# Inverting the 16x16 diagonal blocks of a chunked RWKV-7 recurrence: row by row over sixteen rows, or in two halves of eight

## The chip, the cores and the metric

The kernel runs on one core of one Trainium2 chip. The metric is the device time of one execution in microseconds (us), as the median of several runs. The engines are TensorE (PE; its weight loads are shown as PEld), VectorE (DVE), ScalarE (ACT), GpSimd (POOL) and SyncE (SP), which issues most of the DMAs.

## The reference

The model is a trunk of two layers over 1024 tokens of 1024 channels, all in float32. Layer 0 mixes tokens with a spatial-gating MLP, layer 1 with RWKV-7 time mixing; after each comes a squared-ReLU MLP of width 4096. Only the recurrence of layer 1 is touched here. For 16 heads of 64 channels it computes, token by token,

```
def step(S, inp):
    r_t, w_t, k_t, v_t, a_t, b_t = inp
    sa = einsum('bhij,bhj->bhi', S, a_t)
    S = S * w_t[..., None, :] + sa[..., None] * b_t[..., None, :] + v_t[..., None] * k_t[..., None, :]
    y = einsum('bhij,bhj->bhi', S, r_t)
    return S, y
```

The kernel does this in chunks of 64 tokens. Inside a chunk the tokens depend on each other through a strictly triangular 64x64 matrix L (for each head and chunk), and the chunk needs the inverse of I - L.

## The kernel before, in words

Channels lie on the 128 partitions, tokens along the free axis. The program runs the spatial-gating layer and its MLP, then the RWKV layer, then the last MLP. The products of the RWKV layer (projections to r, k, v, decay, gates, and the output projection) are taken a quarter of the tokens (256) at a time; weights come in pieces of 128x512 (SP queue, L260), are split into a high and a low part (wh: L285 on ACT and DVE; wl: L291 on DVE and POOL) and multiplied in `gemm_steps` (L803). Inputs of the products are mixes of neighbouring tokens (L787) that are split too (L321 on ACT, L324 on DVE).

Beside these products runs the recurrence (`wkv`). It has 16 units, one for each token quarter and pair of head pairs. A unit is made of stages, each a generator:

- A (`unit_a`) makes decay products, normalized keys (L1182, L1185), the operand `ar` (L1192) and, on PE, the grams (L1204); DVE masks them to `la` and `rr` (L1209). `la` holds L; it goes to a DRAM tile `ltd` (L1213).
- E (`unit_e`) transposes keys and values (L1228, L1238).
- S (`unit_s`, L1247 to L1276) inverts the 16x16 blocks on the diagonal of I - L. The 64 blocks of a unit (half of its 128) lie one to a partition, and in this layout S is work for DVE alone. It loads the blocks to `lb` (L1255) and then, for each row i from 2 to 15, multiplies column i of `lb` with the rows done so far into `pr` (L1263, i x i elements) and sums along the last axis into row i of `tb` (L1265). L1261 does row 1, L1267 makes the transposed copy. Two DMAs take `tb` to the DRAM tile `tpd` (L1271), and four bring it from there to the tiles `t` and `pf` (L1276).
- B (`unit_b`) goes from 16x16 to 32x32 and 64x64 blocks by small matmuls: L1300, a copy on ACT (L1306), L1312 and L1314, then L1319 on DVE and L1322 on ACT, L1329, copies L1334, L1340, copies L1344.
- C (`unit_c`) goes through the four chunks of the unit one after the other: L1366 and L1368, copy L1370, L1379, copies L1381, L1386, and L1394 on DVE, which makes the next state S. L1391 and L1392 make the output, D (`unit_d`) is the group norm (L1412 to L1427).

What stands in which order: each engine executes its instructions in program order and waits on semaphores. The steps of the generators are merged by due time (`interleave`): each yields a time in units, and the background products yield what they take; the table `RATES` says how much background goes beside a unit (20 to 20.6 for most, 8 for three of the last units). The framework then reorders what was emitted by its own estimate of when each instruction is ready. The yields of S run from 0.64 to 0.92, those of B start at 1.34 and those of C at 1.67.

Of the kernel before, what the change touches and what calls it, by code (L numbers as in the profile page):

```python
# [9 lines left out]
F32 = mybir.dt.float32  # L10
# [7 lines left out]
D = 1024  # L18
# [17 lines left out]
class Norm:  # L36
    """1 / rms of some tokens, the squares as the channels come, then what is made of it."""
# [36 lines left out]
    def ahead(self, n, e):  # L74
        """The normed values, to n."""
        self.n = n
        self.k.nc.vector.tensor_tensor(n[:, e], self.x[:, e], self.r, ALU.mult)


class Trunk:  # L80
# [16 lines left out]
    # ---------------------------------------------------------------- setup  # L97
# [18 lines left out]
    def mod(self, l, j):  # L116
        """Steps that make one adaLN vector of layer l, [128, 8], channel = chunk * 128 + partition."""
# [17 lines left out]
    def first_mods(self, l, js, hf):  # L135
        """The same for half of the vectors that all waits for, most of the sums on the tensor engine."""
# [23 lines left out]
    def ada_end(self, l, j, hf, ps):  # L160
        """Half a vector from sums along the free axis, the same on all partitions."""
# [11 lines left out]
    def ada_next(self, ahead=3):  # L173
        """The next block of ada_w; a later one is asked for ahead of its use."""
        while self.ada_todo and len(self.ada_got) < ahead:
            l, j, hf, k = self.ada_todo.pop(0)
            raw = self.aw.tile([P, 512], F32, name="araw", bufs=ahead + 1)
            self.last_ada = self.nc.sync.dma_start(raw, self.a["ada_w"][l, j, k, :, hf * 512:hf * 512 + 512])
            self.ada_got.append(raw)
        return self.ada_got.pop(0)  # L180
# [10 lines left out]
    def tick(self, n=1):  # L191
        """Emit n steps of the work that runs beside the products, norms first."""
# [8 lines left out]
    def flush(self):  # L201
        """Emit all steps of the norms."""
# [10 lines left out]
    # ---------------------------------------------------------------- pieces  # L213
    def acc(self):
        """A PSUM bank for a product."""
# [9 lines left out]
    def std(self, src):  # L225
        """A block of weights, half of the input channels at a time."""
        return [(src[:, h * 4:h * 4 + 4], 1, None) for h in range(2)]

    def stream(self, stop):
        """All weights in the order of use."""  # L230
# [40 lines left out]
    def split_piece(self):  # L271
        """Split weights: w = wh + wl exactly, each of 12 significant bits."""
# [23 lines left out]
    def prepare(self, n):  # L296
        """Have n split pieces ready."""
# [3 lines left out]
    def piece(self, ahead=None):  # L301
        """The next split piece; later ones are split, and others asked for, ahead of use."""
# [10 lines left out]
    def block(self):  # L313
        """The next two pieces, as high and low parts by input chunk."""
# [11 lines left out]
    def gemm(self, ps, w, x):  # L326
        """ps = w^T x, as wh xh + wh xl + wl xh."""
# [10 lines left out]
    # ---------------------------------------------------------------- SGU layer  # L338
# [35 lines left out]
    def v_weights(self, wx, ks):  # L374
        """The next split weights of v, for input chunks ks and half the channels."""
# [6 lines left out]
    def v_product(self, ps, h, tt, ks):  # L382
        """Half the channels of v for a token tile, from input chunks ks."""
# [5 lines left out]
    def sgu_begin(self, h, wx, mods, load):  # L389
        """The first products of v, of input chunks whose modulation is known, while mods makes the others'."""  # L390
# [14 lines left out]
    def sgu(self, h, sp, wx, ps0):  # L405
        """The gated product of both halves, split, in hp; h is let go."""
        nc = self.nc
        # v, tokens on partitions
# [5 lines left out]
        # half the channels at a time  # L414
# [26 lines left out]
        # u, channels on partitions; gating  # L441
# [26 lines left out]
    def sgu_out(self, x, ms, norms):  # L468
        """The output projection, one token half after the other."""
# [10 lines left out]
    # ---------------------------------------------------------------- MLP  # L480
    FB = FC // P

    # the hidden blocks that the first MLP takes last, the first token half before the second
# [8 lines left out]
    def mlp_pieces(self, l):  # L492
        """The weights of an MLP, but for the last of the first one."""
# [11 lines left out]
    def pairs(i):  # L505
        """How many pairs of output blocks the first MLP has left for before job i of the RWKV layer."""
# [30 lines left out]
    def mlp_block(self, l, x, h, fc, second=None):  # L537
        """One block of hidden channels. The first takes the first half of the tokens before the second, whose h
        is seen to by second(n), before step n."""
# [8 lines left out]
    def mlp_first(self, x, h, norms, second, last_up):  # L548
        """x += gate * MLP(h). norms is of what follows, by token half, and made along with the last of it;
        last_up comes when h is done with. Goes on as steps of two output blocks each."""  # L550
# [32 lines left out]
    def mlp_last(self, x, h, norms, second, last_up):  # L583
        """The same for the last layer, with norms by token range. last_up makes room for the weights of the last
        output blocks."""
# [18 lines left out]
    # ---------------------------------------------------------------- norms  # L604
    def modulated(self, l, j, hf, x, h):
        """Norm and modulation of a token half, split, to h[hf]."""
# [19 lines left out]
    def final(self, t0, x, last):  # L626
        """The output from token t0 on."""
# [17 lines left out]
    def prenorm(self, hf, x):  # L645
        """x and its norm for the RWKV layer, to DRAM; that of the first quarter also stays."""
# [15 lines left out]
    def rwkv_setup(self):  # L662
# [12 lines left out]
        # the norm of a key is taken of 2^-16 times its square  # L675
# [8 lines left out]
        # ones on the two diagonal 64-blocks, and what centres within a head  # L684
# [6 lines left out]
        # the same ones, rows scaled by r_k  # L691
# [3 lines left out]
        # gram masks [s, t]: s < t for the columns of alpha, s <= t for those of rho  # L695
        self.gmask = c.tile([P, 2, CS], F32, name="gmask")
        nc.gpsimd.memset(self.gmask, 1.0)
        # 0 for the rows of even 16-blocks, 1 for those of odd ones
# [12 lines left out]
        # 0 where a chunk starts  # L711
# [7 lines left out]
    # ---------------------------------------------------------------- RWKV: products of a token quarter  # L719
# [3 lines left out]
    def jobs(self):  # L723
        """The products in order: two blocks of 128 output channels, the hidden layer of a low-rank pair, or
        all of its outputs."""
# [10 lines left out]
    def parts(self):  # L736
        """The jobs before and beside the recurrence."""
# [5 lines left out]
    def pieces(self, jobs):  # L743
        """What the products take of the weights, in the order of use, half of the input channels at a time."""
# [30 lines left out]
    def mixes(self):  # L775
        """The token-shift mixes, split, one channel block at a time, in the order of use."""
# [17 lines left out]
    def gemm_steps(self, ps, x):  # L794
        """ps = w^T x in pieces, with the weights next in line."""
# [13 lines left out]
    def mix_set(self):  # L809
        """The next set of eight mixes; makes what is missing of it."""  # L810
# [5 lines left out]
    def ahead(self, n=1):  # L816
        """Make mixes of the next set."""
# [4 lines left out]
    def acc2(self):  # L822
        """A bank for two blocks."""
# [17 lines left out]
    def hidden(self, q, name, _):  # L841
# [15 lines left out]
        for m in (P, 96):  # L857
# [3 lines left out]
            # sigmoid(z) = 0.5 tanh(z / 2) + 0.5  # L861
# [38 lines left out]
    def gated(self, q, i):  # L900
        """What the output projection takes of a unit, split."""
# [8 lines left out]
    def outp(self, q, _, m):  # L910
        """Two blocks of the output projection of one token quarter, and the residual."""
# [27 lines left out]
    def last_outp(self, x, h, done=None):  # L939
        """Half of the output projection of the last token quarter, the first or the last four input chunks,  # L940
        added to x in place."""
# [16 lines left out]
    def rwkv_open(self):  # L958
        nc = self.nc
        N = self.N  # L960
        # first h of a token quarter, its step from token to token and small temporaries, then x of the first half
# [18 lines left out]
    def mt(self):  # L980
        """A small temporary."""
# [12 lines left out]
    def open_s(self):  # L994
        """For the hidden channels of an MLP, and h of the first quarter of the RWKV layer."""
# [4 lines left out]
    def rwkv(self, steps, before):  # L1000
        """The layer but for the output of the last quarter; the first steps of it beside those of steps."""
# [25 lines left out]
    # Chunk matrices in DRAM: rows of 64, a chunk every CB, so that 16-blocks on the diagonal follow at BB.  # L1027
# [599 lines left out]
```

## Time and profile before

| | |
|---|---|
| median of 3 runs | 2887.13 us (2882.05 to 2897.93) |
| the profiled execution, span from first to last instruction | 2884.1 us |
| PE busy in the span | 2724.9 us (94%) |
| DVE busy in the span | 1743.7 us (60%) |
| ACT busy, POOL busy | 1116.4 us (39%), 579.9 us (20%) |

The profile is of one execution, and for it the page shows no time but the span; the median of the runs is 3.0 us above that. "Busy" is the time in which an engine executes; a row of a view that ends in "<-" names what released the engine after it had been idle. The recurrence and its background products fill the stretch from about 1180 to 2110 us of the span. [...]

### The profile page before, as it was taken

The numbers are of one execution on the slowest core, as the hardware profiler recorded it, in microseconds if no ns is written. First come the engines' busy times: TensorE is split into PE (matmuls) and PEld (weight loads), VectorE is DVE, ScalarE is ACT, GpSimd is POOL, SyncE is SP. The second block draws the span as 40 slices with busy tenths as digits, with TensorE's granted clock in tenths as the row PEclk, the third lists the DMA queues.
The fourth block names the chain that finished last, engine by engine and source line by source line (L and its number), as shares of the span: only waits on it lengthen the run. The fifth ranks groups of instructions, "written<-read, shape, count | busy, mean of one in ns | idle before, by whom it ended". The sixth has DMA issues, their size and how long they took to land.

```text
span 2884.1 us, 48457 instructions
## 1 busy us (share of the span) xinstructions
PE 2724.9 (94%) x18858; PEld 2237.1 (78%) x18858; DVE 1743.7 (60%) x3315; ACT 1116.4 (39%) x2094; POOL 579.9 (20%) x568
## 2 busy tenths in 40 slices
PE   6999999999999998888899988998989999999998
PEld 4788888888888777777777777776778888888887
DVE  7856865433334577788888888677766333333335
ACT  4523432211222445445555555555454222122224
POOL 1000000000000033645544554554410000000002
PEclk9999999999999999888998989899999999999999
DMA  7644544111112446655555545545552111111112
GB/s 273 214 134 136 172 131 133 59 48 48 48 48 73 143 129 202 198 162 152 147 157 159 152 140 149 145 143 160 160 182 88 48 48 48 48 51 48 48 47 71
DMA packets 309414, 342.02 MB, mean 119 GB/s; under 512 B 150464, under 2 KB 165824, under 8 KB 308416
## 3 DMA queue, kind: packets, MB, share of 16 engines
q1 hardware_dynamic: 294208, 312.59, 36.0%
q10 hardware_dynamic: 14976, 26.34, 2.5%
q8 instruction: 148, 2.42, 0.3%
q14 instruction: 82, 0.67, 0.1%
HBM read 286.39 MB, written 52.45 MB: 117 GB/s over the span
## 4 chain that ended last, share of the span: by engine, by line
PE 73%; DVE 14%; DMA 4%; ACT 3%; issue 3%; POOL 1%; SPq 0%; DVEq 0%; ACTq 0%; POOLq 0%
PE acc L332 31%; PE acc L531 24%; PE acc L803 6%; PE acc L387 2%; DVE pr L1263 2%; DVE wl L291 2%; DVE xi L324 2%; DVE hm L787 2%; PE acc L888 1%; DVE ar L1192 1%; DMA araw<-in_ada_w 1%; PE g L1204 1%; PE m L1204 1%; DVE wh L285 1%; PE acc L952 1%
## 5 line engine op out<-in xcount | busy, mean ns | idle before, releaser
L332 PE MATMUL acc<-h,wh 128*128 128x512 f32 x2560 | 804.0, 395 | 0.6 <-ACT h L321 0.3
L285 ACT CAST wh<-raw 128x512 fp32r<-128x512 f32 (+1 forms) x589 | 362.5, 618 | 978.3 <-PE acc L531 533.2
L531 PE MATMUL acc<-s,wh 128*128 128x512 f32 (+1 forms) x2112 | 644.6, 387 | 0.6 <-DVE wh L285 0.6
L332 PEld LDWEIGHTS acc<-h,wh 128*128 128x128 f32 x2560 | 478.5, 188 | 114.4 <-DVE h L324 1.4
L291 DVE TENSOR_TENSOR wl<-raw,wh 128x512 fp32r<-128x512 f32 x524 | 379.1, 726 | 215.2 <-ACT wh L285 211.3
L332 PE MATMUL acc<-h,wl 128*128 128x512 f32 x1280 | 505.6, 395 | 0.0
L803 PE MATMUL acc<-xi,wh 128*128 128x256 f32 (+1 forms) x2176 | 469.9, 311 | 6.4 <-ACT xi L321 3.6
L531 PEld LDWEIGHTS acc<-s,wh 128*128 128x128 f32 x2112 | 393.2, 189 | 89.4 <-DVE s L323 0.9
L531 PE MATMUL acc<-s,wl 128*128 128x512 f32 (+1 forms) x1056 | 411.4, 390 | 0.5 <-DVE wl L291 0.5
L803 PEld LDWEIGHTS acc<-xi,wh 128*128 128x128 f32 (+1 forms) x2176 | 363.3, 202 | 32.9 <-issue 6.5
L336 DVE SCALAR_TENSOR_TENSOR x<-acc,mod,x 128x512 f32<-128x512 f32 (+1 forms) x232 | 165.1, 712 | 310.7 <-PE acc L531 294.5
L803 PE MATMUL acc<-xi,wl 128*128 128x256 f32 (+1 forms) x1088 | 325.0, 299 | 12.2 <-POOL wl L291 7.9
L291 POOL TENSOR_TENSOR wl<-raw,wh 128x512 fp32r<-128x512 f32 (+1 forms) x164 | 233.2, 1424 | 304.1 <-ACT wh L285 171.2
L332 PEld LDWEIGHTS acc<-h,wl 128*128 128x128 f32 x1280 | 240.6, 188 | 54.1 <-issue 0.5
L803 PEld LDWEIGHTS acc<-xi,wl 128*128 128x128 f32 (+1 forms) x1088 | 219.0, 201 | 17.4 <-POOL wl L291 8.9
L531 PEld LDWEIGHTS acc<-s,wl 128*128 128x128 f32 x1056 | 199.1, 189 | 42.9 <-DVE wl L291 1.2
L323 DVE CAST s<-relu 128x512 fp32r<-128x512 f32 x128 | 54.6, 426 | 224.1 <-ACT relu L519 224.1
L517 ACT ACTIVATE relu<-acc 128x512 f32<-128x512 f32 x128 | 76.0, 594 | 210.0 <-PE acc L332 210.0
L656 POOL TENSOR_SCALAR hq<-nt,mod,mod 128x256 f32<-128x256 f32 x8 | 5.9, 742 | 747.8 <-DVE nt L654 747.7
L640 POOL TENSOR_TENSOR hm<-hm,rstd 128x512 f32<-128x512 f32 x8 | 10.9, 1402 | 720.6 <-ACT rstd L638 720.6
L1263 DVE TENSOR_TENSOR pr<-lb,tb 64x4 f32<-64x4 f32 (+6 forms) x224 | 109.1, 487 | 3.1
L126 DVE SCALAR_TENSOR_TENSOR ada_acc<-araw,cond,ada_acc 128x512 f32<-128x512 f32 x140 | 104.3, 746 | 9.4 <-DMA araw<-in_ada_w 7.7
(233 smaller groups left out, 3570.1 us busy)
## 6 DMA issues: line engine op xcount, KB each, us to landing
raw<-in_mlp_w SPq DMA_DIRECT2D x304, 256.0 KB, 2.6
araw<-in_ada_w SPq DMA_DIRECT2D x192, 256.0 KB, 3.6
raw<-in_w_in SPq DMA_DIRECT2D x192, 256.0 KB, 3.1
raw<-in_b_w_out SPq DMA_DIRECT2D x64, 256.0 KB, 3.5
raw<-in_a_w_out SPq DMA_DIRECT2D x32, 256.0 KB, 2.8
raw<-in_w_v SPq DMA_DIRECT2D x24, 256.0 KB, 4.5
x<-in_x SPq DMA_DIRECT2D x4, 1024.0 KB, 6.9
raw<-in_w_u SPq DMA_DIRECT2D x16, 256.0 KB, 3.3
```

The source lines that it names most:

```text
L126: nc.vector.scalar_tensor_tensor(acc, raw, self.cond[:, k:k + 1], acc, ALU.mult, ALU.add)
L285: (nc.vector.tensor_copy if self.nhi % 3 == 0 and self.shared else nc.scalar.copy)(wh[:rows], raw[:rows])
L291: eng.tensor_tensor(wl[:rows], raw[:rows], rd(wh[:rows]), ALU.subtract)
L324: nc.vector.tensor_tensor(lo, src, rd(hi), ALU.subtract)
L332: nc.tensor.matmul(ps, w[s](k), x[m][:, k], start=n == 0, stop=n == 3 * KC - 1)
L336: self.nc.vector.scalar_tensor_tensor(x[:, e], ps, gate[:, e:e + 1], x[:, e], ALU.mult, ALU.add)
L387: self.nc.tensor.matmul(ps, h[s][:, k, ts], self.wv[k][m], start=k + i == 0, stop=k + i == KC + 1)
L517: nc.scalar.activation(r, ps, AF.Relu)
L531: nc.tensor.matmul(ps, w[:, k], s[hf, k][:, i, ts], start=n == 0, stop=n == 3 * FB - 1)
L787: nc.vector.scalar_tensor_tensor(t, self.hx[:, e], self.mu[:, i, e:e + 1], self.h[:, e, 1:], ALU.mult, ALU.add)
L803: nc.tensor.matmul(ps, s[:, k], xk[:, i], start=n == 0, stop=n == 23)
L1263: V.tensor_tensor(pr[:, :i, :i], lb[:, 0:i, i].unsqueeze(1).to_broadcast([64, i, i]), tb[:, 0, 0:i, 0:i].rearrange("p s k -> p k s"), ALU. ...
```

## The change

S is written in halves. The two 8x8 blocks on the diagonal of a 16x16 block are inverted together: for each row i from 2 to 7, one multiplication (L1275) of 2 x i x i elements and one sum (L1276). Then the 8x8 block below them is made as two products, each a multiplication of 8x8x8 = 512 elements (L1281, L1285) and a sum (L1283 into a new tile `wd`, L1287 into `tb`). Each unit so has 16 multiplications and sums where it had 28. The first copy (now L1272) and the transposing copy (now L1289) are still there. `pr` has 512 elements where it had 256. The other lines of the diff only take comments out; lines after S are 22 further down in the new file (L1300 is L1322, L1366 is L1388).

```diff
-        pr = self.ups[0].tile([64, NB, NB], F32, name="pr")
+        H = NB // 2
+        pr = self.ups[0].tile([64, H * H * H], F32, name="pr")
+        wd = self.ups[0].tile([64, H, H], F32, name="wd")
+
+        def halves(t, rows, cols):
+            return bass.AP(tensor=t.tensor, offset=t.offset, ap=[t.ap[0], [H * NB + H, 2], *rows, *cols])
+
         yield 0.64
-        for i in range(1, NB):
+        T = tb[:, 0]
+        for i in range(1, H):
+            row = bass.AP(tensor=T.tensor, offset=T.offset + i * NB, ap=[T.ap[0], [H * NB + H, 2], [1, i]])
+            col = bass.AP(tensor=lb.tensor, offset=lb.offset + i, ap=[lb.ap[0], [H * NB + H, 2], [0, i], [NB, i]])
             if i == 1:
-                V.tensor_copy(tb[:, 0, 1, 0:1], lb[:, 0, 1:2])
+                V.tensor_copy(row, col[:, :, 0])
                 continue
-            V.tensor_tensor(pr[:, :i, :i], lb[:, 0:i, i].unsqueeze(1).to_broadcast([64, i, i]),
-                            tb[:, 0, 0:i, 0:i].rearrange("p s k -> p k s"), ALU.mult)
-            V.tensor_reduce(tb[:, 0, i, 0:i], pr[:, :i, :i], AX.X, ALU.add)
-            yield 0.64 + .017 * i
+            out = pr[:, :2 * i * i].rearrange("p (b k s) -> p b k s", b=2, k=i)
+            V.tensor_tensor(out, col, halves(T, [[1, i]], [[NB, i]]), ALU.mult)
+            V.tensor_reduce(row, out, AX.X, ALU.add)
+            yield 0.64 + .022 * i
+        out = pr.rearrange("p (r k s) -> p r k s", r=H, k=H)
+        cube = [64, H, H, H]
+        V.tensor_tensor(out, lb[:, :H, H:].rearrange("p s r -> p r s").unsqueeze(2).to_broadcast(cube),
+                        T[:, :H, :H].rearrange("p s k -> p k s").unsqueeze(1).to_broadcast(cube), ALU.mult)
+        V.tensor_reduce(wd, out, AX.X, ALU.add)
+        yield 0.85
+        V.tensor_tensor(out, T[:, H:, H:].unsqueeze(2).to_broadcast(cube),
+                        wd.rearrange("p s k -> p k s").unsqueeze(1).to_broadcast(cube), ALU.mult)
+        V.tensor_reduce(T[:, H:, :H], out, AX.X, ALU.add)
+        yield 0.89
         V.tensor_copy(tb[:, 1], tb[:, 0].rearrange("p s k -> p k s"))
         yield 0.92
```

The new yields move what is emitted, and the framework's reordering follows. On DVE, the end of S in the second unit stood so before (`pr`, `tb` and `lb` are S's tiles, `wh`, `wl` and `raw` are weights of the background products):

```order
L1265 TENSOR_REDUCE tb_9783<-pr 64x12
L1263 TENSOR_TENSOR pr<-lb,tb_9783 64x13x13
L1265 TENSOR_REDUCE tb_9783<-pr 64x13
L1263 TENSOR_TENSOR pr<-lb,tb_9783 64x14x14
L1265 TENSOR_REDUCE tb_9783<-pr 64x14
L1263 TENSOR_TENSOR pr<-lb,tb_9783 64x15x15
L291 TENSOR_TENSOR wl<-raw,wh 128x512
L1265 TENSOR_REDUCE tb_9783<-pr 64x15
L285 CAST wh<-raw 128x512
L1267 COPY tb_9783<-tb_9783 64x256
```

and stands so now, with the next instructions of stage A behind it:

```order
L1281 TENSOR_TENSOR pr<-lb,tb_9783 64x512
L285 CAST wh<-raw 128x512
L1283 TENSOR_REDUCE wd<-pr 64x64
L291 TENSOR_TENSOR wl<-raw,wh 128x512
L1285 TENSOR_TENSOR pr<-tb_9783,wd 64x512
L1287 TENSOR_REDUCE tb_9783<-pr 64x8x8
L1289 COPY tb_9783<-tb_9783 64x256
L291 TENSOR_TENSOR wl<-raw,wh 128x512
L285 CAST wh<-raw 128x512
L291 TENSOR_TENSOR wl<-raw,wh 128x512
L1182 SCALAR_TENSOR_TENSOR k<-rn,k 128x512
```

The instructions of the background that stood inside S here now stand partly behind it; from the first copy to the last there are 41 instructions before in the third unit, 25 now.

On PE, the order of units 1 to 12 is the same but for small moves (B of the first unit stands 19 background matmuls earlier, of the ninth 12). In the last units it isn't. Stage B of the last unit stood so before (`acc` is a product of the background, `t<-t` the first step of B, `t<-pf,w` its second, `c` is stage C):

```order
L803 MATMUL acc<-xi,wh 128x256 x2
L803 MATMUL acc<-xi,wl 128x256
L1300 MATMUL t<-t,la_20657 32x16 x30
L803 MATMUL acc<-xi,wl 128x256
L803 MATMUL acc<-xi,wh 128x256 x2
L803 MATMUL acc<-xi,wl 128x256
L1366 MATMUL c<-uv_20656,la_20657 64x64
L1368 MATMUL c<-st_7852,ar_9786 64x64
L1368 MATMUL c<-st_7853,ar_9786 64x64
L1366 MATMUL c<-uv_20656,la_20657 64x64 x2
L1312 MATMUL t<-pf_21405,w_21660 16x16 x2
```

and stands so now (L1322 is the old L1300, L1334 the old L1312, L1434 the old L1412 of stage D):

```order
L803 MATMUL acc<-xi,wh 128x256
L803 MATMUL acc<-xi,wl 128x256
L803 MATMUL acc<-xi,wh 128x256 x2
L803 MATMUL acc<-xi,wl 128x256
L1322 MATMUL t<-t,la_20492 32x16 x32
L1434 MATMUL r<-ysq,bones 128x512
L1334 MATMUL t<-pf_21229,w_21484 16x16 x2
L803 MATMUL acc<-xi,wh 128x256 x2
L803 MATMUL acc<-xi,wl 128x256
L803 MATMUL acc<-xi,wh 128x256
L1334 MATMUL t<-pf_21229,w_21484 16x16 x2
```

B of the last three units stands 31, 44 and 49 background matmuls earlier than before, and with fewer of them between its steps.

## Rows read from the trace of the kernel before

**Rows 1.** Three stretches: busy us (instructions) by engine, PEclk, DMA share, GB/s

```profile
1180.00:2110.00 930.00, 831.59 (x10139) 693.26 (x10139) 738.70 (x1666) 484.48 (x1021) 468.49 (x445) 0.91 0.55 156
0.00:1180.00 1180.00, 1140.70 (x5176) 921.14 (x5177) 678.86 (x1119) 403.84 (x684) 87.36 (x101) 0.98 0.39 126
2110.00:2884.10 774.10, 752.60 (x3548) 622.70 (x3546) 326.15 (x532) 228.05 (x390) 24.09 (x24) 0.99 0.20 62
```

**Rows 2.** PE's waits, 1180 to 2110: us in total, times, longest

```profile
PE g L1204 <- DVE ar L1192: 21.8, 12, 4.2
PE c L1366 <- DVE S L1394: 19.3, 13, 3.7
PE t L1340 <- ACT w L1334: 12.5, 8, 2.9
```

**Rows 3.** The chain that ended last, 1180 to 2110, by line

```profile
by line: PE acc L803 16.7%; issue 7.8%; DVE pr L1263 5.1%; DVE ar L1192 4.1%; PE acc L888 3.9%; DVE xi L324 3.4%; PE g L1204 3.3%; DVE hm L787 3.2%; DVE wl L291 3.1%; PE m L1204 2.4%; PE c L1366 2.2%; PE c L1368 2.1%; PE c L1379 1.9%; DVE w
```

**Rows 4.** Stretches of 10 us about S of the first unit, columns as in rows 1

```profile
1250.00:1260.00 10.00, 3.77 (x11) 2.20 (x10) 10.00 (x21) 4.32 (x12) 9.29 (x6) 0.75 0.39 131
1260.00:1270.00 10.00, 10.00 (x41) 6.81 (x40) 8.63 (x24) 2.74 (x6) 1.84 (x1) 0.50 0.49 158
```

**Rows 5.** DVE busy in S's multiplications (first row) and sums, 1180 to 2110

```profile
1180.00:2110.00 930.00, 109.10 (x224) 0.91 0.55 156
...
1180.00:2110.00 930.00, 51.87 (x224) 0.91 0.55 156
```

**Rows 6.** Groups of DVE instructions by shape: busy us, mean ns, idle before

```profile
L1263 DVE TENSOR_TENSOR pr<-lb,tb 64x225 f32<-64x225 f32 x16 | 11.0, 685 | 0.3
L1263 DVE TENSOR_TENSOR pr<-lb,tb 64x81 f32<-64x81 f32 x16 | 9.4, 587 | 0.3
L1263 DVE TENSOR_TENSOR pr<-lb,tb 64x100 f32<-64x100 f32 x16 | 8.2, 513 | 0.1
L1263 DVE TENSOR_TENSOR pr<-lb,tb 64x49 f32<-64x49 f32 x16 | 7.6, 478 | 0.3
L1265 DVE TENSOR_REDUCE tb<-pr 64x15 f32<-64x225 f32 x16 | 6.0, 375 | 0.2
L1263 DVE TENSOR_TENSOR pr<-lb,tb 64x9 f32<-64x9 f32 x16 | 5.7, 356 | 0.2
L1263 DVE TENSOR_TENSOR pr<-lb,tb 64x36 f32<-64x36 f32 x16 | 4.6, 286 | 0.3
L1265 DVE TENSOR_REDUCE tb<-pr 64x10 f32<-64x100 f32 x16 | 3.9, 242 | 0.2
L1263 DVE TENSOR_TENSOR pr<-lb,tb 64x16 f32<-64x16 f32 x16 | 3.3, 208 | 0.1
L1265 DVE TENSOR_REDUCE tb<-pr 64x3 f32<-64x9 f32 x16 | 2.4, 148 | 0.2
```

**Rows 7.** Timeline of DVE, eighth unit: start us, us, engine, line

```profile
1656.25 0.50 DVE L1263 TENSOR_TENSOR pr<-lb,tb 64x196 f32<-64x196 f32 x1
1656.79 0.35 DVE L1265 TENSOR_REDUCE tb<-pr 64x14 f32<-64x196 f32 x1
1657.17 1.51 DVE L1263 TENSOR_TENSOR pr<-lb,tb 64x225 f32<-64x225 f32 x1
1658.71 0.38 DVE L1265 TENSOR_REDUCE tb<-pr 64x15 f32<-64x225 f32 x1
```

**Rows 8.** Timeline of POOL, same place

```profile
1656.99 1.28 POOL L291 TENSOR_TENSOR wl<-raw,wh 128x512 fp32r<-128x512 f32 x1 [2.89 <-ACT wh L285]
```

**Rows 9.** DVE's waits, 1180 to 2110, columns as in rows 2

```profile
DVE uv L1381 <- PE c L1379: 21.5, 21, 4.0
DVE k L1182 <- ACT rn L1178: 14.1, 9, 3.5
```

**Rows 10.** Timeline of the last unit: load of `pf`, first matmuls of B

```profile
2083.63 1.26 SPq L1276 DMA_DIRECT2D pf<-tpd  x2
2087.43 0.24 PE L1300 MATMUL t<-t,la 16*32 16x16 f32 x4
```

## The prediction, made before the changed kernel was run

> **What bounds the kernel now.** I read the busy times by stretch first [rows 1]. Outside the recurrence PE is busy all but 39 us of 1180 and 22 us of 774; nothing on DVE can be worth much there. In the recurrence (1180 to 2110) PE is busy 831.6 of 930 us, so 98.4 us are idle, and its clock is 0.91 of full where the other stretches have 0.98 and 0.99. [...] DVE is busy there 738.7 us, 79%.
>
> Second, PE's own waits in that stretch [rows 2]. The two largest end on DVE: the grams wait for L1192 (21.8 us, 12 times) and stage C for the new state, L1394 (19.3 us, 13 times). No row has PE waiting for S itself. S costs PE time in another way: DVE executes in program order, and L1192 and L1394 stand behind or between S's instructions.
>
> Third, the chain that ended last [rows 3]. S's multiplications are its largest DVE entry, 5.1% of 930 = 47 us. They are busy 109.1 us in all [rows 5], so 43% of their time lies on the chain. Fourth, a look at ten-microsecond stretches about the first S [rows 4]: DVE is busy 10.0 of 10, PE 3.77, and in the next stretch PE's clock is 0.50. A burst on DVE is paid twice, once as a stall and once as a slow clock after it.
>
> **The change part by part.** It removes, for each of 16 units, 14 multiplications and 14 sums, together 109.10 + 51.87 = 160.97 us [rows 5].
>
> It adds six small multiplications of 8, 18, 32, 50, 72 and 98 elements. Taking the row of the nearest old size for each [rows 6]: 0.356 (9), 0.208 (16), 0.286 (36), 0.478 (49), 0.587 (81), 0.513 (100), together 2.43 us. These means contain the delays by POOL that the sizes show unevenly, so single terms are rough and the sum is better. The six small sums lie between the rows for 9 and 100 elements, 0.148 and 0.242; six times the middle, 0.195, is 1.17 us.
>
> It adds two multiplications of 512 elements and two sums of 512. The sums are the safe term: from 9 to 225 elements they go from 0.148 to 0.375, 1.05 ns an element, so 512 take 0.375 + 287 x 1.05 ns = 0.68 us each, 1.35 for two. For the multiplication no row comes near 512. Undelayed, one of 196 elements took 0.50 us where the sum of 196 took 0.35 [rows 7]: the reading by strides of 16 elements costs 0.15/196 = 0.77 ns an element more, 1.82 in all. From the mean for 225, 0.685, that gives 0.685 + 287 x 1.82 ns = 1.21 us. From below it is bounded by the sum of 512, 0.68. From above: the one of 225 elements that began while POOL was at a 1.28 us subtraction took 1.51 us [rows 7, 8], some 0.96 more than the 0.55 that 196 and 1.82 ns an element give, and if each long one met that it would take 0.50 + 316 x 1.82 ns + 0.96 = 2.04 us. I take 1.21, near the measured mean of 225, so 2.41 us for two.
>
> A unit then has 2.43 + 1.17 + 1.35 + 2.41 = 7.36 us, 16 units 117.8 us; DVE is relieved of 160.97 - 117.8 = 43 us, with the bounds of the long multiplication 43 + 32 x 0.53 = 60 and 43 - 32 x 0.83 = 16 us. To that come gaps: an instruction of S that needs the one just before it starts 30 to 40 ns after that one's end [rows 7]. Twelve fewer such steps in 16 units are 12 x 16 x 0.035 = 7 us at most. I take 48 us in all, 3 us a unit.
>
> [...]
>
> [...]
>
> What costs nothing: the first and the last copy of S stay; `wd` and the longer `pr` are space alone; the same six DMAs follow. SP's weight loads are queued behind L1271, which waits for the last copy; that comes earlier now, if anything.
>
> **From DVE time to the span.** 48 us at 43% on the chain is 21 us. Not all of it can come through, since DVE also waits for PE inside this stretch: L1381 for stage C 21.5 us, L1182 for ACT 14.1 us [rows 9]. Where S was filling such a wait, its going shortens nothing. I take 60%, 13 us. The clock: 84 us lost against 98 idle is 0.85 for each idle us. If it follows in proportion 13 us give 11 more; I take half, 6. That is 19 us of the span, 2884.1 - 19 = 2865, and with the 3 us by which the median of the runs stands above the profiled execution 2868 us.
>
> **The rivals.**
>
> *Much more comes back.* The two waits on DVE [rows 2] go altogether, since in each unit DVE reaches L1192 and L1394 3 us sooner and the mean wait is 1.8 and 1.5 us: 41 us, and with the clock in proportion 35 more, 2887 - 76 = 2811; half of it 2849. For it: the mean wait is smaller than what a unit gains. Against: some of these waits lie away from any S, and C's own chain of PE, ACT and DVE sets when L1394 can start.
>
> *Nothing comes through.* S only fills DVE's waits for PE; PE's order hardly changes in the first twelve units, so its stalls stay where stage C's own hand-overs set them. The time is 2882 to 2892. For it: PE never waits for S by name, DVE has 191 us idle. Against: S on the chain [rows 3] and the burst of [rows 4].
>
> *Slower, by the last units.* There the new order puts stage B 31 to 49 background matmuls earlier and leaves less between its steps: in the last unit one matmul stands between L1322 and L1334, which need an ACT copy between them, where nine stood. B has five such hand-overs a unit; the one row that shows their price when uncovered is L1340 behind the copy L1334, 12.5 us in 8 waits, 1.56 each [rows 2]. In the last four units 20 of them cost up to 31 us. It also wants the block sooner: before, `pf` was asked for at 2083.6 and B began at 2087.4 [rows 10], which leaves little to give. Against a gain of 14 (three quarters of 19) in the first twelve units that makes 2887 + 17 = 2904. It decides if more than half of these hand-overs are uncovered. Against it: the matmuls that no longer stand there stand later and cover other waits, and S ends earlier too.
>
> That the change doesn't do what it says can be left out: the order shows 16 multiplications and sums a unit.
>
> **How the numbers follow.** The forecast case, a gain of 7 to 32 us (2855 to 2880), has 0.47; the larger gain 0.15; nothing 0.24; slower 0.14. About 0.5% (14.4 us) is what a measurement can tell from no change: below 2872.7 is faster, above 2901.6 slower. Three quarters of the forecast case lie below 2872.7, so faster has 0.35 + 0.15 = 0.50, within 0.5% 0.12 + 0.24 = 0.36, slower 0.14. The range for 8 in 10 takes the forecast case, nothing, and the nearer part of the other two: 2843 to 2898.
>
> **What the profile after would show.** Right: S's multiplications and sums together near 118 us instead of 161, the long multiplications at a mean of about 1.2 us; DVE in the recurrence near 692 us; the waits of L1192's and L1394's readers on PE (now L1204 and L1388) together some 10 us smaller; the granted clock of the stretch a little above 0.91. Wrong: long multiplications near 2 us; DVE relieved as said with PE's idle time the same; or new waits in the last four units between B's steps (now L1334, L1351, L1362) that take back more than 10 us.

## The result, and the profile after

The changed kernel takes 2904.9 us (median of 17 runs, 2899.1 to 2919.2), the kernel before, measured along with it, 2888.0 (17 runs). The ratio is 1.0058, with a 95% interval of 1.0039 to 1.0077: slower, where 2868 us and a gain were forecast. The time lies above the forecast range (2843 to 2898) too. Three executions in all, of two kernels of the experiments (3876 and 6067 us of `new_s_old_order`, 11450 us of `new_order_last_4`), ran far longer than the rest of their kernel and stand in no ratio.

The same three stretches of the profile after (span 2897.4 us), columns as in [rows 1]; PEclk is the TensorE clock that was granted, as a share of full speed (in the profile before it is 1.00 from 1288 to 1291 us and 0.50 from 1264 to 1267):

```profile
1180.00:2110.00 930.00, 822.52 (x9952) 685.76 (x9953) 706.01 (x1457) 480.39 (x1011) 459.11 (x438) 0.90 0.53 151
0.00:1180.00 1180.00, 1138.14 (x5182) 918.95 (x5182) 680.33 (x1121) 405.10 (x685) 88.89 (x102) 0.99 0.40 127
2110.00:2884.00 774.00, 764.53 (x3719) 633.58 (x3718) 327.88 (x536) 230.84 (x396) 28.67 (x28) 0.99 0.21 65
```

Ahead of the recurrence hardly anything changed. Inside it DVE is busy 32.7 us less, and PE did less too, 822.5 us instead of 831.6: with less on DVE, PE stood idle 107.5 us instead of 98.4, at a clock of 0.90 instead of 0.91. What it had not done by 2110 us stands in the last stretch, 764.5 instead of 752.6.

S's own time on DVE fell as was summed. The largest groups of S by shape, 1180 to 2110 us (busy us, mean ns):

```profile
L1281 DVE TENSOR_TENSOR pr<-lb,tb 64x512 f32<-64x512 f32 x16 | 21.8, 1365 | 0.2
L1285 DVE TENSOR_TENSOR pr<-tb,wd 64x512 f32<-64x512 f32 x16 | 21.3, 1333 | 0.0
L1283 DVE TENSOR_REDUCE wd<-pr 64x64 f32<-64x512 f32 x16 | 10.8, 674 | 0.2
L1287 DVE TENSOR_REDUCE tb<-pr 64x64 f32<-64x512 f32 x16 | 10.7, 669 | 0.1
...
L1289 DVE COPY tb<-tb 64x256 f32<-64x256 f32 x16 | 8.9, 554 | 0.1
```

All 16 shapes of multiplications and sums add up to 117.9 us; 117.8 were forecast, and before it was 161.0. DVE's whole busy time in the span fell by less, 24.8 us (1743.7 to 1718.9): the two copies of S took back 5.5 us, and the rest, other instructions and the overlap of neighbouring records, which busy time counts once, was not taken apart. PE's waits in the same stretch show where the relief didn't arrive:

```profile
PE c L1388 <- DVE S L1416: 21.2, 10, 3.9
PE g L1204 <- DVE ar L1192: 16.7, 10, 4.5
PE t L1362 <- ACT w L1356: 15.0, 9, 3.0
PE c L1408 <- ACT uv L1403: 10.8, 7, 5.7
```

Against [rows 2], the grams wait 5.1 us less for `ar`, as forecast. Stage C does not: it waits 1.9 us more for the state update, and 10.8 us for ACT's copy of `uv`, a wait of 2.0 us before. DVE in turn waits longer for C; for the first row [rows 9] had 21.5 us, and the last row here is the kernel before, for the second:

```profile
DVE uv L1403 <- PE c L1401: 35.7, 26, 7.1
DVE S L1416 <- PE c L1408: 28.2, 19, 4.8
...
DVE S L1394 <- PE c L1386: 8.7, 13, 2.2
```

One of the ten stalls at L1388 shows how it comes about. DVE in the third unit (start us, us, engine, line, idle before):

```profile
1365.67 1.25 DVE L787 SCALAR_TENSOR_TENSOR hm<-hm,mu 128x256 f32<-128x256 f32 x1 [1.13 <-POOL hm L785]
1366.85 2.12 DVE L1285 TENSOR_TENSOR pr<-tb,wd 64x512 f32<-64x512 f32 x1
1368.89 0.27 DVE L1416 SCALAR_TENSOR_TENSOR S<-c,g,sg 128x64 f32<-128x64 f32 x1
1369.09 0.67 DVE L1287 TENSOR_REDUCE tb<-pr 64x64 f32<-64x512 f32 x1
1369.68 0.27 DVE L1416 SCALAR_TENSOR_TENSOR S<-c,g,sg 128x64 f32<-128x64 f32 x1
```

and PE at the same place, first what the updates need, then who waits for them:

```profile
1363.31 0.45 PE L1408 MATMUL c<-uv,tm 128*64 128x64 f32 x8
...
1370.09 0.48 PE L1388 MATMUL c<-uv,la 64*64 64x64 f32 x4 [3.87 <-DVE S L1416]
```

The matmuls that the updates read were done at 1363.8 us. PE then made C's output and background products for 2.5 us and stood still for 3.9. In front of the first update stands one of S's long products (2.12 us, with POOL busy beside it; of the 32 in this trace the six that met no work of POOL took 1.02 to 1.17, and of those that met some 15 took 1.03 to 1.14 and eleven 1.24 to 2.15), and between the first and the second one of its long sums. DVE took them in the order in which they are issued, though the matmuls had been done for 3.1 us when the long product began, so the next chunk of C starts behind both. Seven of the stalls at L1388 over 1.3 us, together 18.9 us, look like this.

### The profile page after: what moved, and what is told of

Same layout as the page of the kernel before. It is cut to its first block, busy times and chain, and to the rows that moved or that the text cites. A ratio compares the mean times of both kernels' runs of the same rounds, so it can differ in the third digit from the quotient of the medians.

```text
span 2897.4 us, 48265 instructions
## 1 busy us (share of the span) xinstructions
PE 2727.1 (94%) x18858; PEld 2239.3 (77%) x18858; DVE 1718.9 (59%) x3123; ACT 1117.8 (39%) x2094; POOL 578.1 (20%) x568
## 5 line engine op out<-in xcount | busy, mean ns | idle before, releaser
L531 PEld LDWEIGHTS acc<-s,wl 128*128 128x128 f32 x1056 | 198.5, 188 | 42.3 <-DVE wl L291 0.9
L324 DVE TENSOR_TENSOR xi<-hm,xi 128x256 fp32r<-128x256 f32 x192 | 103.3, 553 | 5.2 <-ACT xi L321 4.6
```

Source lines behind the costliest of these rows:

```text
L324: nc.vector.tensor_tensor(lo, src, rd(hi), ALU.subtract)
L531: nc.tensor.matmul(ps, w[:, k], s[hf, k][:, i, ts], start=n == 0, stop=n == 3 * FB - 1)
```

## The experiments

Two devices serve all of them. In a kernel with a *forced order*, each engine issues in an order given by a table; the instructions stay the same (the comment is added here):

```diff
             Trunk(tc, aps, out, ctx).run()
+        keep_order(nc, tc)      # an ordering edge from each instruction to the next of its engine in a table
```

"Old order" is that of before, "new order" that of the changed kernel. No run forces a kernel into its own order and changes nothing else; the nearest is `new_order_first_12` below, forced, at 1.0059 where the changed kernel, not forced, has 1.0058. And every ratio is to the kernel before, from five rounds, with its 95% interval; where a profile is quoted, it is a single execution. Profiles of one order differ: `new_s_old_order` and `new_order_last_4` issue alike up to unit 13, and reached the grams of unit 12 11 us apart. So verdicts go by the ratios, and a wait read from one profile is a hint.

### What DVE's time in S is worth

`s_small` is the kernel before in its own order with S's multiplications and sums on 2x2 elements alone (most of S's arithmetic is left out); `s_heavy` makes each product of S twice.

```diff
-            V.tensor_tensor(pr[:, :i, :i], lb[:, 0:i, i]..., tb[:, 0, 0:i, 0:i]..., ALU.mult)
-            V.tensor_reduce(tb[:, 0, i, 0:i], pr[:, :i, :i], AX.X, ALU.add)
+            V.tensor_tensor(pr[:, :2, :2], lb[:, 0:2, i]..., tb[:, 0, 0:2, 0:2]..., ALU.mult)      # s_small
+            V.tensor_reduce(tb[:, 0, i, 0:2], pr[:, :2, :2], AX.X, ALU.add)
+            V.tensor_tensor(two, ..., ALU.mult)            # s_heavy: two = [64, 2, i, i], the same product twice
+            V.tensor_reduce(tb[:, 0, i, 0:i], two[:, 0], AX.X, ALU.add)
```

> The kernel before in its own order, but each multiplication and sum of S works on 2x2 elements only (most of S's arithmetic is left out, the instruction count is the same). DVE is relieved of about 161 - 14 x 16 x (0.25 + 0.143) = 73 us. Theory A: with 43% of it on the chain a gain of some 15 to 30 us, ratio 0.990 to 0.995. Rival B: also a gain, at least 0.3%. Rival C: 1.000 within 0.002.

> The kernel before in its own order, but each multiplication of S makes its products twice (2 x i x i elements), so DVE has 1239 x 1.82 ns x 16 = 36 us more in instructions of up to 0.95 us. Theory A: 43% of it, 10 to 20 us slower, ratio 1.003 to 1.007. Rival B: more than A, since the instructions are also longer: 1.006 to 1.012. Rival C: 1.000 within 0.002.

Measured: `s_small` 0.9905 (0.9873 to 0.9937), `s_heavy` 1.0074 (1.0048 to 1.0101). PE's wait for the state update moved with them, from 19.5 us (1180 to 2150) to, in `s_small` (the first row is the same matmul, with its wait put down to a sum of S):

```profile
PE c L1366 <- DVE tb L1265: 6.7, 3, 2.5
...
PE c L1366 <- DVE S L1394: 3.0, 2, 2.8
```

and in `s_heavy` (its lines are one further down):

```profile
PE c L1367 <- DVE S L1395: 30.2, 21, 3.4
```

In the profiles S's multiplications and sums take 106.4 us in `s_small` and 196.1 us in `s_heavy`, 161.0 before. `s_small` was expected to take off 73 us and took off 54.6 (its multiplications of 2x2 elements took 0.33 us in the mean, not 0.25). So S's time on DVE counts when the order stays, in both directions: 27 us for 54.6 us less (50%, by the interval 33 to 67%), 21 us for 35.1 us more (61%, 40 to 83%). `s_small` lies where theory A had it, `s_heavy` above A's range and inside that of B, and its interval holds both. The rival that nothing comes through has fallen, and the prediction's 19 of 48 us, 40%, is within the first interval and at the edge of the second.

### The order and the size, apart

`new_s_old_order` issues the changed kernel's instructions in the old order: the small rows in the places of their rows, the long products and sums in those of rows 9, 10, 13 and 14. `old_s_new_order` issues the old instructions in the new order, rows 8 to 15 two at a time where the long instructions stand.

> The changed kernel's instructions, each engine forced to issue in the order of the kernel before; the 18 instructions of S stand in slots of the old 30 (small rows in their own slots, the long products in those of rows 9, 10, 13 and 14, the transposing copy in its own). Theory A (the new issue order costs more than the relief of DVE gives): ratio to before 0.993 to 0.998 (2868 to 2882 us). Rival B (the long instructions of 1.3 us on DVE hold up stage C whatever the order): 1.003 to 1.010. Rival C (S's cost counts for nothing, only order does): 1.000 within 0.002. DVE busy in S about 118 us in all three.

> The instructions of the kernel before, forced to issue in the order of the changed kernel; rows 8 to 15 of S stand, two at a time, where the four long instructions stand. Theory A: slower than the changed kernel, ratio to before 1.008 to 1.015. Rival B: 1.000 to 1.003, since the long products are gone. Rival C: 1.006, as the changed kernel.

Measured: 0.9979 (0.9955 to 1.0002) and 1.0159 (1.0132 to 1.0186). The changed instructions alone do no harm and may gain 0.2%; the order alone costs 1.6% with the old S, more than theory A expected, and 0.8% with the new one (1.0058 against 0.9979). The loss against before goes with the order. The missing gain does only in part: in the old order S takes 36.8 us less than before (124.2 us), and the 40% of the prediction would make 15 us of it, 0.9949; measured are 6 us, and the interval ends at 0.9955.

### Which units

`new_order_last_4` has the old order to the start of unit 13 and the new one from there; `new_order_first_12` the reverse.

> The changed kernel's instructions in the old order up to the start of unit 13 and in the new order from there on. Theory T (the rival of the prediction: the last four units carry the loss): 1.004 to 1.008, as the changed kernel. Theory U (the new order loses a little in every unit): 0.999 to 1.002, that is the 0.998 of the old order and a quarter of the loss of 0.8%.

> The changed kernel's instructions in the new order up to the start of unit 13 and in the old order from there on. Theory T: 0.997 to 1.000. Theory U: 1.002 to 1.005.

Measured: 1.0000 (0.9977 to 1.0023) and 1.0059 (1.0037 to 1.0080). The loss comes with the new order of the first twelve units, where PE's order hardly moved. In the last four it costs at most little: 1.0000 against the 0.9979 of `new_s_old_order`, with intervals that overlap. The rival of the prediction that ended slower named the last four units: it had the sign right and the place wrong.

### S's places, or the rest

`new_order_old_places` is the new order, but S's instructions have as many others ahead of them on DVE as in the old one; `old_order_new_places` the old order with S at its new places; `new_s_old_order_soon` is `new_s_old_order` with the long products and sums 1 to 4 places earlier, and nothing else moved.

> The changed kernel with every instruction in its own (new) order, except that on DVE each instruction of S stands behind as many others as it did in the order of the kernel before. Theory P (where S stands among the state updates of stage C on DVE makes the new order dear): ratio to before 0.997 to 1.001, and PE's wait of stage C for the state update back from 21 us to about 18. Rival Q (the new order of everything else makes it dear): 1.004 to 1.008, as the changed kernel.

> The changed kernel's instructions in the old order, except that S on DVE stands behind as many others as in the new order. Theory P: 1.003 to 1.008. Rival Q: 0.996 to 0.999, as with the old places or a little better, since the end of S comes sooner.

> The changed kernel's instructions, every engine in the order of before as in new_s_old_order (0.9979), but S's long products and sums in the slots of the rows just behind the sixth small one, so some 1 to 4 DVE places earlier, only the last copy in its own. If only the amount of S's work counts: 0.997 to 0.999. If a long product that stands where a short one did delays what is queued behind it (state updates, ar): 1.001 to 1.008. If an S that ends early helps stage B: 0.992 to 0.996.

Measured: 1.0147 (1.0125 to 1.0169), 1.0128 (1.0104 to 1.0152) and 1.0171 (1.0132 to 1.0210). Neither S's places nor the others' order is bad by itself, so both theories of the first two fell: each mixture is worse than either whole order. The third says it most plainly: the same instructions, moved by a few places on one engine, cost 1.9% (1.0171 against 0.9979), more than any theory expected. The waits name two sides. Too early, and C stands behind S, here with the long instructions one after another ahead of a pair of updates, more than between the two; PE's waits in `new_s_old_order_soon` (1180 to 2160):

```profile
PE c L1388 <- DVE S L1416: 29.4, 11, 5.5
PE g L1204 <- DVE ar L1192: 19.4, 13, 2.6
PE t L1362 <- ACT w L1356: 16.3, 9, 2.8
PE c L1408 <- ACT uv L1403: 12.7, 9, 4.4
```

Too late, and stage B stands waiting for the block that S made; PE's waits in `new_order_old_places`, a row that before doesn't have, and C's update at 11.0 us (1180 to 2160):

```profile
PE t L1322 <- DMA t<-tpd: 24.6, 7, 6.8
...
PE c L1388 <- DVE S L1416: 11.0, 9, 1.9
```

### Is the new order a bad draw?

The framework makes its order by its own estimate of when each instruction is ready, so any edit may deal another. Two kernels make S's last copy as two of 128 elements, one only states S's steps earlier (two edits in one block, the comments added here):

```diff
-        V.tensor_copy(tb[:, 1], tb[:, 0].rearrange("p s k -> p k s"))
+        for h in (slice(0, 8), slice(8, 16)):      # before_copy_in_halves, after_copy_in_halves
+            V.tensor_copy(tb[:, 1, h], tb[:, 0, :, h].rearrange("p s k -> p k s"))
-            yield 0.64 + .022 * i
+            yield 0.64 + .017 * i                  # after_steps_early; and 0.79, 0.83 for 0.85, 0.89
```

> The kernel before, S's last copy alone made as two copies of 128 elements; one instruction more in a unit, at most 0.3 us each, 5 us of DVE in all, which by the 0.74% that 36 us more cost is 0.1%. The framework's own order comes out different on every engine (4923 rows of difference on PE, 2364 on DVE). Theory D (the framework's order is a draw: any small edit deals all engines a new one, and that is worth up to about 1% either way): at least 0.4% off 1.001, more likely above, 1.005 to 1.012. Theory N (the orders it makes are equally good for instructions it is fed, and only the new S's long instructions make a bad one): 1.000 to 1.003.

> The changed kernel, S's last copy alone made as two copies, in the order that the framework then makes. Theory D: a new draw, anywhere from 0.992 to 1.012, and more than 0.3% away from the 1.0058 of the changed kernel. Theory N: the long instructions stand in it as in the changed kernel, 1.004 to 1.009.

> The changed kernel, not an instruction different; S's steps are only said to come earlier in a unit (0.017 for 0.022 a row, the long products at 0.79 and 0.83 for 0.85 and 0.89). The order is the same to the middle of the recurrence and differs behind it (1383 rows of PE, 865 of DVE). Theory D: 0.3% or more off 1.0058 either way (less than a full draw, since half of it is the same). Theory N: 1.0040 to 1.0075.

Measured: 0.9996 (0.9971 to 1.0021), 0.9977 (0.9954 to 1.0000) and 1.0068 (1.0044 to 1.0093). The first is no test: most of the rows of difference that its expectation counts are line numbers that the edit shifts. In the traces, without line numbers, 71 of 18858 matmuls stand elsewhere (two profiles of one order on PE differ in some 30), 47 instructions on DVE, the 16 added ones among them, 10 on ACT and none on POOL, so its order is nearly the old one. The second is: 583 matmuls, 392 instructions on DVE (with the 16 added ones), 143 on ACT and 48 on POOL stand elsewhere than in the changed kernel, from the first units on, and 0.8% came back. The new S is not bound to a bad order. The third has the changed kernel's order through the first six units and another one behind them, and its time within 0.1%: theory N had that, theory D did not. So not every new draw pays differently.

### The state updates first

By then 14 kernels allowed a comparison: PE's waits of three kinds, for the state update, for the copies of `uv` and for S's block, went with the time. The three kinds were picked with these times in view. Here is the table, with the four kernels that followed from it at its end (us of one profiled execution, 1180 to 2230):

| kernel | ratio | update | `uv` | block | sum |
|---|---|---|---|---|---|
| s_small | 0.9905 | 3.0 | 3.8 | 0 | 6.8 |
| after_copy_in_halves | 0.9977 | 23.3 | 3.1 | 0 | 26.4 |
| new_s_old_order | 0.9979 | 18.0 | 6.2 | 0.8 | 25.0 |
| before_copy_in_halves | 0.9996 | 18.7 | 3.8 | 0 | 22.5 |
| before | 1 | 19.5 | 2.0 | 0 | 21.5 |
| new_order_last_4 | 1.0000 | 15.9 | 8.4 | 0 | 24.3 |
| after | 1.0058 | 21.2 | 10.8 | 0 | 32.0 |
| new_order_first_12 | 1.0059 | 18.3 | 10.5 | 0.7 | 29.5 |
| after_steps_early | 1.0068 | 21.9 | 7.0 | 0 | 28.9 |
| s_heavy | 1.0074 | 30.2 | 6.4 | 0 | 36.6 |
| old_order_new_places | 1.0128 | 29.8 | 8.4 | 0 | 38.2 |
| new_order_old_places | 1.0147 | 11.0 | 14.0 | 24.6 | 49.6 |
| old_s_new_order | 1.0159 | 38.2 | 13.6 | 0 | 51.8 |
| new_s_old_order_soon | 1.0171 | 29.6 | 12.7 | 0 | 42.3 |
| *then:* new_order_c_first | 0.9991 | 8.1 | 12.8 | 0 | 20.9 |
| before_c_first | 0.9981 | 13.7 | 5.0 | 0 | 18.7 |
| old_order_c_first | 0.9962 | 13.5 | 5.9 | 0 | 19.4 |
| copy_halves_c_first | 0.9949 | 11.7 | 8.2 | 0 | 19.9 |

A straight line through all 18 has 0.064% of the time, 1.9 us, for each us of such waiting (correlation 0.95, single kernels up to 0.5% off it). It does not hang on the choice alone: in `s_small` 8.1 us more of the update's wait are put down to S's rows, and with such waits counted in every kernel the correlation is 0.93; PE's whole idle time in the stretch gives 1.8 us for each us, and 0.96. The granted clock fell along (0.93 from 1180 to 2110 in `new_s_old_order`, 0.87 in `new_s_old_order_soon`).

A correlation shows no cause, so the four kernels make one edit, on DVE alone: where instructions of S stand between the two updates of a step of C, or one right ahead of the first, they go behind the second. In `new_order_c_first` these are 11 places and 22 instructions; one of them:

```diff
 L1245 TENSOR_TENSOR v_9781<-g,v_9781 128x256
+L1416 SCALAR_TENSOR_TENSOR S<-c,g_9796,sg 128x64 x2
 L1285 TENSOR_TENSOR pr<-tb_9784,wd 64x512
-L1416 SCALAR_TENSOR_TENSOR S<-c,g_9796,sg 128x64
 L1287 TENSOR_REDUCE tb_9784<-pr 64x8x8
-L1416 SCALAR_TENSOR_TENSOR S<-c,g_9796,sg 128x64
```

> The changed kernel in its own order but for 11 places on DVE: where one of S's two long products or their sums stands between the two state updates of a step of stage C (or right ahead of the first), it now stands right behind the second; 22 instructions of S move by 2 or 3 places, nothing else moves on any engine. Theory C (the loss is what C's hand-overs wait for: over the 14 kernels so far PE's waits for the state update, for the uv copies and for S's block, 21.5 us before, 32.0 in the changed kernel, 49.6 and 51.8 in the two near 1.015, go with the time at 0.063% a us): seven of the changed kernel's stalls at L1388 hold one or two long instructions, some 1.5 us each, so the waits fall by 8 to 12 us and the time to 0.998 to 1.002. Rival D (the order as a whole, no single place): 1.004 to 1.008. Rival T (S's block is what B waits for, and S now ends later): 1.006 or more, with PE waits for the DMA of the block.

> The same edit on the changed kernel's instructions in the old order (new_s_old_order, 0.9979): 14 places, 14 instructions of S behind the pair of updates. Theory C: its waits of C for the state update, 18.0 us, fall by 4 to 8, the time to 0.992 to 0.996. Rival D: 0.9965 to 1.000. Rival T: 1.000 or more.

> The same edit on the kernel with the last copy in halves, in that kernel's own order (0.9977): 8 places. Theory C: its waits of C for the state update, 23.3 us, fall by 5 to 10, the time to 0.991 to 0.996. Rival D: 0.9965 to 1.000. Rival T: 1.000 or more.

> The kernel before in its own order, with the edit of new_order_c_first: in 35 places on DVE one or two of S's row instructions stand between the two state updates of a step of C (or right ahead of the first) and now stand right behind the second. Theory C: the state update waits of PE, 19.5 us, fall by 6 to 12, the time to 0.993 to 0.998 at 0.063% a us; the new S is then worth only the rest of what copy_halves_c_first (0.9949) and old_order_c_first (0.9962) gained, 0 to 0.3%. Rival L (only the long instructions harm a pair; the old rows of 0.1 to 0.7 us between the updates are too short): 0.998 to 1.001, and the gain of the two kernels is the new S's.

Measured: `new_order_c_first` 0.9991 (0.9971 to 1.0011), clear of the changed kernel's 1.0058 (1.0039 to 1.0077). Twenty-two instructions moved by two or three places took back the whole loss against before; both rivals expected 1.004 or more. Its PE waits (1180 to 2160):

```profile
PE c L1408 <- ACT uv L1403: 12.8, 9, 5.2
PE acc L803 <- POOL wl L291: 9.3, 5, 4.7
PE c L1388 <- DVE S L1416: 8.1, 8, 2.1
```

The update's wait fell from 21.2 to 8.1 us, the `uv` copies' did not, and no wait for S's block came, so S ending later cost nothing. At the place shown above, which comes some 8 us later in this execution, DVE now goes

```profile
1376.05 1.25 DVE L787 SCALAR_TENSOR_TENSOR hm<-hm,mu 128x256 f32<-128x256 f32 x1 [1.14 <-POOL hm L785]
1377.22 0.46 DVE L1416 SCALAR_TENSOR_TENSOR S<-c,g,sg 128x64 f32<-128x64 f32 x2
1377.61 1.78 DVE L1285 TENSOR_TENSOR pr<-tb,wd 64x512 f32<-64x512 f32 x1
```

and PE

```profile
1377.83 0.33 PE L1388 MATMUL c<-uv,la 64*64 64x64 f32 x4 [1.23 <-DVE S L1416]
```

Both updates stand ahead of the long product, and PE's stall here is 1.23 us instead of 3.87.

`old_order_c_first` gave 0.9962 (0.9938 to 0.9987), between theory C's 0.996 and rival D's 0.9965, with an interval that holds both; its wait for the update fell by 4.5 us. `copy_halves_c_first` gave 0.9949 (0.9924 to 0.9974), where theory C had it, with the wait down by 11.6 us. At 2874.5 us it is the fastest kernel of the study that makes all of S, faster than before and than the changed kernel. `before_c_first` gave 0.9981 (0.9955 to 1.0008), at the border of its two theories, with the wait down by 5.8 us where at least 6 were expected. So what the best two gain is partly the place of the updates and partly S's halves, some 0.2 to 0.3% each by these numbers; the intervals overlap and the split stays open.

Two things keep this from being the whole account of the new order. The same edit is worth 0.7% there and 0.2 to 0.3% in the three other kernels, and after it the new order still stands behind the two that also have the new S (0.9991 against 0.9962 and 0.9949), though each of these ratios is uncertain by 0.2 to 0.3%. And the number of such places does not tell the orders apart: counted by the same rule, long instructions stand between or right ahead of two updates in 12 places of the changed kernel, in 14 of `new_s_old_order` and in 13 of `after_copy_in_halves`, and the last has a longer wait for the update than the changed kernel (23.3 us). What makes the same places dearer in the new order is not shown; its longer waits for `uv` are in the table.

## Why the prediction was wrong

*What bounds the kernel* was right. The loss and all gains lie in the recurrence, in PE's waits there. A us of S's rows is worth about what the chain of [rows 3] said, or more: 43% against the 50 and 61% of `s_small` and `s_heavy`, whose intervals hold it.

*The cost of S* was right: 117.9 us for 117.8. It was not right in each term. The long multiplications took 1.35 us where 1.21 was taken, 1.02 to 1.17 with POOL idle and 1.03 to 2.15 beside it, inside the bounds for the mean; the sums of 512 took 0.67 us for 0.68 (669 and 674 ns in the mean), and the small multiplications together 2.2 us a unit for 2.43. The first long product reads both operands at steps of 64 bytes, the second one of them at step one, and they took alike (from 1020 and from 1053 ns), so the 0.77 ns an element that the prediction put down to the steps is not shown to be theirs. A term was missing: the copies, costed at nothing, rose from 379 to 554 ns (L1289) and from 135 to 301 ns (L1272, of two elements where it was one), 5.5 us in 16 units.

*From DVE time to the span* is the step that failed. "48 us at 43% on the chain is 21 us", and the like "in each unit DVE reaches L1192 and L1394 3 us sooner", hold if DVE's other instructions keep their order and S's work can be passed at any point. For L1192 the wait fell, by 5.1 us, but hardly by S alone: with the same S in the old order it is 20.9 us (1180 to 2230), against 21.8. For L1394 (now L1416) it did not, for two reasons that the order showed and the prediction did not use. First, the framework dealt a new order to all engines, and the prediction weighed it for PE in the last units alone. Second, half of S's work now comes in four pieces of 0.67 to 2.1 us that nothing passes. In the old order too S's rows stood between the two updates of a pair or right ahead of the first, in 36 places, but they are short, 0.15 to 0.69 us in the mean [rows 6]; in the new order long pieces stand so in 12. Less work thus stood in worse places, and moving it out of 11 of them gave back the whole 0.7% (1.0058 to 0.9991). Even so hardly anything of the 0.7% that was forecast came (0.9991), and in the old order the new S gave 0.2% of it: the price of a us that `s_small` and the chain have, for many short instructions in their places, does not hold for a few long ones. Which part of that is their length and which the rest of the order is open.

*The clock* followed the idle time, as was said, with the other sign: 0.91 to 0.90, as PE's idle time in the stretch went from 98.4 to 107.5 us. The 84 us that the prediction's sum counts as lost to the clock are the author's estimate, (1 - 0.91) x 930 us from [rows 1]; no run shows them by themselves. The same estimate after, from a clock rounded to 0.90, is 93 us, 0.87 for each idle us where 0.85 was taken, and over the 18 kernels a us of PE's idle time went with 1.8 us of the time.

*The rivals.* Nothing comes through: refuted by `s_small`. Much more: not seen; `s_small`, which takes more off S than the change does (54.6 us), gave 27 us, where this rival had 38 to 76. Slower by the last units: its time, 2904, is what was measured, but `new_order_last_4` stands at 1.0000, so it was right by accident. What was missing among them is a rival on DVE's order in the first twelve units.

*What the profile after would show*: S at 118 us, yes; its long multiplications 1.35 us, not 1.2; DVE in the recurrence 706 us, not 692; the two waits 10 us smaller, no, 41.1 to 37.9; the clock higher, no.

Open: why ACT's copies of `uv` come late in the new order (10.8 us, 12.8 in `new_order_c_first`). No run tried it alone.

## What to carry to other kernels

Work taken off an engine that another waits for was worth its share of the chain here where the order around it stayed and what was left of it could be passed as easily (27 us for 54.6 in `s_small`, but 6 for 36.8 in `new_s_old_order`, which has the long instructions, and 17 us lost in the changed kernel, which has the new order too); when a framework makes the order, look first at which instructions now stand ahead of each hand-over, in all units. Here a few long instructions in place of many short ones saved DVE time and took away gaps in which an urgent small one could pass: put the hand-overs (here a pair of 0.27 us updates) ahead of it explicitly. When a change with the right sum comes out slower, run the new instructions in the old order before doubting the sum.

## What was not expected of the hardware

The transposing copy of 16x16 blocks, the same instruction in both kernels, took 379 ns in the mean before and 554 after: in the trace after, the eight of them that met no work of POOL took 355 to 386 ns, and the four longest, 566 to 1475 ns, all ran while POOL was busy; the other four that met work of POOL took 354 to 370. The long sums took 662 to 690 ns with and without POOL. A us of PE waiting in this stretch went with 1.9 us of the time over 18 kernels. And single executions of one issue order drifted 11 us apart by the twelfth unit, so that a stretch of one profile can't show a few tenths of a per cent.
